# One branch per unit of expert weights, four hi and four lo buffers, and first loads in another order, in a two-layer hybrid decoder trunk

## The chip, the cores and the metric

The kernel runs on one core of one Trainium2 chip, all matrices in float32. The metric is the device time of one launch in microseconds. The core has five engines with their own instruction streams: PE (TensorE, matmuls), DVE (VectorE), ACT (ScalarE), POOL (GpSimd) and SP (SyncE), which here only issues DMA loads. An engine works through its stream in order; between engines there are semaphores only.

## The reference

Two layers. Each normalises x, mixes tokens (a gated delta rule beside a stick-breaking attention), and adds a feed-forward part: a dense SwiGLU in layer 0, a top-2-of-8 mixture of experts in layer 1. Shift, scale and gate of every part come from `silu(c) @ ada_w`. What matters here:

```python
D_MODEL, SEQ, DEPTH, D_FF, N_EXPERTS, TOP_K = 1024, 256, 2, 3584, 8, 2

def moe_swiglu(h, router_w, router_b, w1, w3, w2):
    logits = hf @ router_w + router_b
    top_logit, top_idx = lax.top_k(logits, TOP_K)
    top_w = jax.nn.softmax(top_logit, axis=-1)
    ...   # tokens gathered per expert in blocks of rows
    y = (jax.nn.silu(xb @ w1[e]) * (xb @ w3[e])) @ w2[e]
    ...   # weighted by top_w and summed back per token

def reference(x, c, ada_w, ...):
    c_act = jax.nn.silu(c)
    for l in range(DEPTH):
        mod = c_act @ ada_w[l] + ada_b[l]       # six parts: shift, scale, gate, twice
        x = x + gt1 * hybrid_mixer(rms_norm(x) * (1 + sc1) + sh1, ...)
        x = x + gt2 * (swiglu(h, ...) if l % 2 == 0 else moe_swiglu(h, ...))
    return rms_norm(x, final_norm)
```

## The kernel before

**Stages.** By the trace, the head (first loads, modulation of layer 0) lasts to about 42 us, the mixer of layer 0 to 385, the dense feed-forward to 640, the mixer of layer 1 to 995, routing and the first gather of tokens to 1013, the eight experts to 1950, and the end (last weighting, final norm, store) to 1970. A list scheduler sets the order of the instructions on each engine, by priorities that follow the program's text.

**Head.** ACT loads c (tile `csil`, L145, one float per element of the transfer, since c is laid out with its 1024 values as 128 x 8), takes silu, and loads some small tables: `rows` of layer 0 and of layer 1 (`setup`, L174 to L178) and the router's bias and weights (`rb`, `rw`, L1112 and L1113). SP loads the constants (`cst`, L157), x (L158) and eight pieces of 1 MiB of `ada_w` (L198, tiles `f`). PE multiplies each piece as it comes (L252, after silu of c is there), and what follows from the last piece opens the first large product (L503). Each DMA signals its end on one of eight semaphores that are handed out in turn (DMAHW0 to DMAHW7); a load whose semaphore is still held by an earlier load waits for that one.

**A unit of expert weights** is 1 MiB. Each expert has 42: 28 for up (w1 and w3, `up`), 14 for down (w2, `down`), in blocks of 1024, 1024, 1024 and 512 of the 3584 columns. For each unit SP loads `raw`, ACT casts it in two halves to a rounded copy `hl` (hi, L1267), and DVE subtracts to get the rest, `lo` (L1271). There are 7 buffers of raw (3 + 4), 4 of hi (3 + 1) and 4 of lo. `weights.group()` pops two units that are ready, after issuing two more loads and splits.

**Light and heavy.** An expert with at most 64 tokens is light: PE multiplies raw in float32 with 64 columns of tokens (`few`: L1372 in up, L1454 in down). Any other is heavy: PE multiplies hi by the tokens' hi and lo parts, and lo by their hi part (`heavy`: L1351, L1438, L1443). Which arm runs is decided on PE at run time by a flag per expert (`Light.arms`, L1219), with one branch for two units: 21 per expert. ACT casts and DVE subtracts in either case. Here experts 0, 2, 4 and 6 are heavy and 1, 3, 5 and 7 light; their stretches alternate. All eight flags are read into registers of PE by `values_load` (L1207) in one go ahead of the first gather (L1314, which multiplies the normalised tokens by a selection matrix `pe`).

**Around the units.** While expert e goes through up, expert e's earlier blocks go through down. Between them stand, for each block: `turned` (PE transposes L1412, ACT's copy `t2r` L1416, DVE's `t2r` L1417, and ACT's float32 copy `s`, called g32 in the code, L1420, from a pool `s32` of one buffer); the product of the two up halves on DVE (L1519); at each expert's start `begin`, with PE transposes (L1398), ACT's copy `pte` (L1400) and DVE's `ws` (L1402); for every second expert a gather (L1314, ACT L1325, L1330, DVE L1331). At the very end `finish_last` (L1488 on) weighs the last expert's result.

## Time and profile before

| | |
|---|---|
| runs | 1971.96, 1973.22, 1966.64 us (median 1971.96) |
| profiled execution | 1972.13 us, its span 1970.3 us |
| busy on PE, DVE, ACT | 1823.6, 1599.0, 1283.3 us |
| from HBM | 535 MB, 272 GB/s over the span |

The span is what the profiler saw between the first and the last instruction; the profiled execution's own time is 1.8 us more. Averages over the whole span mix stages with different limits, so the stages are read apart: busy time of each engine in each stretch, what an engine waited for in it, and the chain of waits at the head, at the start of the experts and at the end.

### The profile page before, as it was taken

What the parts mean: (1) busy time and instruction counts of PE and PEld (TensorE: products, weight loads), DVE (VectorE), ACT (ScalarE), POOL (GpSimd) and SP (SyncE); (2) the same over time, 40 slices, a digit from 0 to 9 for tenths busy, and PEclk for the clock granted to TensorE, in tenths of its full rate; (3) what the DMA queues carried; (4) which work ended last, traced back from release to release, by engine and by line L of the source; (5) the groups of instructions that cost most, each with busy time, mean ns of one, the idle gap of its engine ahead of it and who ended that gap; (6) DMA issues with size and microseconds to landing.
All of it is one profiled execution on the core that took longest, in us unless ns stands there. A gap on an engine that the chain in (4) does not pass through costs nothing.

```text
span 1970.3 us, 36475 instructions
## 1 busy us (share of the span) xinstructions
PE 1823.6 (93%) x14868; PEld 1412.8 (72%) x14868; DVE 1599.0 (81%) x1900; ACT 1283.3 (65%) x1842; POOL 80.0 (4%) x88
## 2 busy tenths in 40 slices
PE   5899999999999899999979988999889998899986
PEld 2889989999999789989968733686337863378522
DVE  3778678687666878588668898997989889898998
ACT  2765556454443665556477788877788687886885
POOL 0101000000000101000000002000020001000000
PEclk8999999999999999999989999999899998899998
DMA  8544447688773344555739999999999999999995
GB/s 279 168 155 144 143 153 235 214 288 279 246 260 95 127 153 131 162 171 193 259 140 377 365 402 348 380 369 365 381 355 383 367 370 365 370 374 368 377 403 232
DMA packets 220334, 539.24 MB, mean 274 GB/s; under 512 B 13602, under 2 KB 120548, under 8 KB 206052
## 3 DMA queue, kind: packets, MB, share of 16 engines
q1 hardware_dynamic: 215216, 536.02, 74.7%
q8 instruction: 148, 2.42, 0.5%
q10 hardware_dynamic: 4916, 0.35, 0.2%
q14 instruction: 54, 0.44, 0.1%
HBM read 535.27 MB, written 1.06 MB: 272 GB/s over the span
## 4 chain that ended last, share of the span: by engine, by line
PE 63%; DVE 18%; ACT 8%; issue 7%; DMA 4%; DVEq 0%; SPq 0%; ACTq 0%
PE g L1351 15%; PE g L379 7%; PE g L375 7%; PE g L377 7%; DVE lo L1271 7%; PE a L1438 4%; PE g L1372 3%; ACT hl L1267 3%; DMA raw<-in_moe_w_dram 2%; PE a L1454 2%; PE a L1443 2%; DVE t L627 2%; DVE hl L340 2%; ACT hl L339 1%; PE a L1055 1%
## 5 line engine op out<-in xcount | busy, mean ns | idle before, releaser
L1271 DVE TENSOR_TENSOR lo<-raw,hl 128x2048 fp32r<-128x2048 f32 (+1 forms) x338 | 754.1, 2272 | 46.5 <-ACT hl L1267 46.4
L1267 ACT CAST hl<-raw 128x1024 fp32r<-128x1024 f32 x672 | 657.3, 1052 | 26.0 <-DMA raw<-in_moe_w_dram 21.6
L340 DVE TENSOR_TENSOR hl<-raw,hl 128x1024 fp32r<-128x1024 f32 (+1 forms) x252 | 298.1, 1188 | 136.8 <-ACT hl L339 136.4
L339 ACT CAST hl<-raw 128x1024 fp32r<-128x1024 f32 (+1 forms) x252 | 256.8, 1022 | 201.3 <-PE g L379 134.0
L375 PE MATMUL g<-r,hl 128*128 128x256 f32 x1536 | 235.2, 293 | 6.6 <-ACT r L483 3.4
L377 PE MATMUL g<-r,hl 128*128 128x256 f32 x1536 | 228.6, 288 | 0.0
L379 PE MATMUL g<-r,hl 128*128 128x256 f32 x1536 | 223.9, 287 | 0.4 <-DVE hl L340 0.4
L1351 PE MATMUL g<-hl,r 128*128 128x512 f32 x896 | 222.9, 391 | 0.0
L375 PEld LDWEIGHTS g<-r,hl 128*128 128x128 f32 x1536 | 204.2, 194 | 15.2 <-ACT r L483 4.7
L1372 PE MATMUL g<-raw,x 128*64 128x512 f32 (+1 forms) x1024 | 212.1, 563 | 0.0
L377 PEld LDWEIGHTS g<-r,hl 128*128 128x128 f32 x1536 | 204.6, 195 | 3.0 <-issue 2.5
L379 PEld LDWEIGHTS g<-r,hl 128*128 128x128 f32 x1536 | 202.6, 194 | 2.6 <-issue 1.9
L1351 PEld LDWEIGHTS g<-hl,r 128*128 128x128 f32 x896 | 167.4, 188 | 37.0 <-ACT hl L1267 2.4
L1372 PEld LDWEIGHTS g<-raw,x 128*64 128x64 f32 x1024 | 71.5, 141 | 114.6 <-issue 104.2
L1454 PE MATMUL a<-raw,s 128*64 128x512 f32 x448 | 120.2, 684 | 3.6 <-ACT s L1420 3.2
L1351 PE MATMUL g<-lo,r 128*128 128x512 f32 x448 | 120.7, 391 | 0.5
L1416 ACT CAST t2r<-a 128x512 fp32r<-128x512 f32 x56 | 32.8, 585 | 113.1 <-PE a L1412 113.1
L1351 PEld LDWEIGHTS g<-lo,r 128*128 128x128 f32 x448 | 83.6, 188 | 20.0 <-DVE lo L1271 2.9
L210 DVE SCALAR_TENSOR_TENSOR f<-raw,csil,f 128x1024 f32<-128x1024 f32 x70 | 92.5, 1322 | 5.7 <-DMA raw<-in_ada_w_dram 5.2
L1438 PE MATMUL a<-hl,t2r 128*128 128x512 f32 x224 | 89.0, 397 | 1.7 <-ACT hl L1267 1.7
L1454 PEld LDWEIGHTS a<-raw,s 128*64 128x64 f32 x448 | 34.3, 157 | 74.5 <-issue 67.3
L1443 PE MATMUL a<-hl,t2r 128*128 128x512 f32 x224 | 87.5, 390 | 0.0
(334 smaller groups left out, 2211.6 us busy)
## 6 DMA issues: line engine op xcount, KB each, us to landing
raw<-in_moe_w_dram SPq DMA_DIRECT2D x334, 1024.0 KB, 7.0
raw<-in_w_in_dram SPq DMA_DIRECT2D x60, 1024.0 KB, 5.4
raw<-in_ffn_w_dram SPq DMA_DIRECT2D x42, 1024.0 KB, 5.8
raw<-in_ada_w_dram SPq DMA_DIRECT2D x40, 1024.0 KB, 5.3
f<-in_ada_w_dram SPq DMA_DIRECT2D x8, 1024.0 KB, 8.6
raw<-in_w_up_dn_dram SPq DMA_DIRECT2D x8, 1024.0 KB, 5.1
raw<-in_w_out_dram SPq DMA_DIRECT2D x8, 1024.0 KB, 5.0
raw<-in_w_up_sb_dram SPq DMA_DIRECT2D x4, 1024.0 KB, 5.1
```

The lines of the kernel that those rows point to most:

```text
L339: A.copy(hv, part)
L340: V.tensor_sub(lv, part, hv.bitcast(F32))
L375: T.matmul(pv[:, b, :], hv[:, k, :], xh[:, k, :], start=(k == 0), stop=False)
L377: T.matmul(pv[:, b, :], hv[:, k, :], xl[:, k, :], start=False, stop=False)
L379: T.matmul(pv[:, b, :], lv[:, k, :], xh[:, k, :], start=False, stop=(k == kc - 1))
L1267: A.copy(hi[:, h, :], raw[:, h, :])
L1271: V.tensor_sub(lo[:, h, :], raw[:, h, :], hi[:, h, :].bitcast(F32))
L1351: T.matmul(ps, x_[:, kk, :], w[:, k, 512 * b : 512 * b + 512], start=(kk == 0 and x_ is xh and w is hv), stop=(kk == KC - 1 and w is lv),)
L1372: T.matmul(banks[0][h, 0:half], x32[:, kk, :], w[:, k, half * i : half * i + half], start=(wide and kk == 0), stop=(kk == KC - 1), skip_gr ...
L1438: T.matmul(ye[nb], gh[:, gs], w[:, k, nw], start=(first and q == 0 and u == 0 and p == 0), stop=(last and u == 1 and p == 3),)
L1443: T.matmul(ye[nb], gl[:, gs], w[:, k, nw], start=False, stop=False)
L1454: T.matmul(ye[nb][h, :], g32[:, gs], w[:, k, 512 * nb : 512 * nb + 512], start=False, stop=(last and u == 1 and k == 1), skip_group_check= ...
```

## The change

In words, in the order of the program:

- c is loaded as 8 rows of 128 floats (`crow`), and PE turns it after silu; `cst` is the first load on SP, x follows two pieces of `ada_w` as before.
- The small `rows` loads of layer 1 and the router's two loads keep their place in the program (`tc.keep_in_program_order`) instead of being moved ahead by the scheduler; `rows` comes from a pool that is shared.
- At the experts' start seven loads are asked for ahead instead of five. The weights of the mixture (`mix`) are computed after the first gather instead of in `route`. The selection slots take one DVE operation instead of two.
- Each flag is read by a call in `begin(e)`.
- `take()` pops one unit, after one load and one split: each unit has a branch of its own (42 per expert). `step()`, which advances gathers and finishing work, runs after every second unit.
- `pte` and `ws` are made by `slots(e)` at the end of the expert's up phase, ahead of its last block's down, instead of at its start, from one buffer; `s32` has two.

```diff
@@ -89,7 +89,7 @@
     phase_m = dict(r8=4, r4=2, f8=7, f4=6, t2=6, i2=5, s2=4)
     banks_m = dict(g=2, s=2, a=3, v=1)
     phase_f = dict(raw2=3, hl2=3, r8=2, f4=4, t2=4, t2r=4)
-    phase_b = dict(raw2=4, hl2=1, lo=4, r4=6, x32=3, s32=1, t2=5, t2r=6, gt=1, xn=2, pe=2, pte=2)
+    phase_b = dict(raw2=4, hl2=1, lo=4, r4=6, x32=3, s32=2, t2=5, t2r=6, gt=1, xn=2, pe=2, pte=1)
 
     layout_b = dict(
         t2r=[P, 512], x32=[P, KC, P // 2], s32=[P, 512], xn=[P, 2, D], pe=[P, 512], r4=[P, KC, P], t2=[P, 512], pte=[P, S], gt=[P, D], raw2=[P, 2048],
...
@@ -142,10 +142,12 @@
 
 
     csil = pc.tile([P, KC], F32, tag="csil", name="csil")
-    nc.scalar.dma_start(csil, c_in[0].rearrange("(k p) -> p k", p=P))
-    A.activation(csil, csil, AF.Silu)
+    crow = pc.tile([KC, P], F32, tag="crow", name="crow")
+    nc.scalar.dma_start(crow, c_in[0].rearrange("(k p) -> k p", p=P))
+    A.activation(crow, crow, AF.Silu)
     cst = pc.tile([P, _CST.shape[1]], F32, tag="cst", name="cst")
     first = CST["i32"][1]
+    nc.sync.dma_start(cst[:, :first], cst_in[:, :first])
     C = {k: cst[:, a:b] for k, (a, b) in CST.items()}
     ident = C["ident"]
     ones = pc.tile([P, P], F32, tag="ones", name="ones")
@@ -154,7 +156,6 @@
     x = pc.tile([P, 2, D], F32, tag="x", name="x")
 
     def load_rows():
-        nc.sync.dma_start(cst[:, :first], cst_in[:, :first])
         nc.sync.dma_start(x, x_in[0].rearrange("(b p) d -> p b d", p=P))
 
...
 
     def setup(l):
 
-        rows = pc.tile([P, 2, P], F32, tag="rows", name=f"rows{l}")
+        pin = tc.keep_in_program_order if l else lambda ins: ins
+        rows = mk("t2", [P, 512])[:, 0 : 2 * P].rearrange("p (i c) -> p i c", c=P)
         G.memset(rows, 0.0)
-        nc.scalar.dma_start(rows[0:48, 0, :], ada_b[l].rearrange("(r p) -> r p", p=P))
...
+        pin(nc.scalar.dma_start(rows[0:48, 0, :], ada_b[l].rearrange("(r p) -> r p", p=P)))
+        pin(nc.scalar.dma_start(rows[48:56, 0, :], norm_mix[l].rearrange("(r p) -> r p", p=P)))
+        pin(nc.scalar.dma_start(rows[56:64, 0, :], norm_ffn[l].rearrange("(r p) -> r p", p=P)))
+        pin(nc.scalar.dma_start(rows[64:65, 0, :], dn_out_norm[l : l + 1, :]))
+        pin(nc.scalar.dma_start(rows[0:96, 1, :], conv_w[l].rearrange("j (r p) -> (j r) p", p=P)))
...
     def ada_first(l, mods):
 
         cs = mk("r4", [P, 4 * S])[:, : 32 * KC].rearrange("p (k c) -> p k c", c=32)
-        V.tensor_copy(cs, csil.unsqueeze(2).broadcast_to([P, KC, 32]))
...
@@ -240,8 +241,12 @@
                 raws[m, q] = ada_load(l, m, q, "f8")
                 if len(raws) == 2:
                     load_rows()
-                if len(raws) == 5:
+                if len(raws) == 4:
                     rest = setup(0)
+        ps = bank("a")
+        T.transpose(ps[:, 0:KC], crow, ident[0:KC, 0:KC])
+        V.tensor_copy(csil, ps[:, 0:KC])
+        V.tensor_copy(cs, csil.unsqueeze(2).broadcast_to([P, KC, 32]))
...
-            nc.scalar.dma_start(rb, router_b[j : j + 1, :].partition_broadcast(P))
-            nc.scalar.dma_start(rw[:, 0], router_w[j].rearrange("(k p) n -> p k n", p=P))
+            tc.keep_in_program_order(nc.scalar.dma_start(rb, router_b[j : j + 1, :].partition_broadcast(P)))
+            tc.keep_in_program_order(nc.scalar.dma_start(rw[:, 0], router_w[j].rearrange("(k p) n -> p k n", p=P)))
...
         light = Light(rt[:, 5, 0])
-        wgt = sm([P, 2, 2])
...
-        V.tensor_add(wt, wt, tmp)
-        return oa, wt, pos, light
+        def mix():
+
+            wgt = sm([P, 2, 2])
...
+            V.tensor_tensor(tmp, tmp, wgt[:, :, 1:2].broadcast_to([P, 2, NE]), ALU.mult)
+            V.tensor_add(wt, wt, tmp)
+
...
             V.tensor_copy(self.int, self.flag)
-            self.back = pc.tile([P, NE], F32, tag="back", name="back")
-            V.tensor_scalar(self.back, self.flag, -float(P // 2), None, ALU.mult)
-            self.regs = [
-                nc.values_load(self.int[0:1, e : e + 1], engines=[mybir.EngineType.PE], min_val=0, max_val=1)
-                for e in range(NE)
-            ]
+            self.regs = {}
 
         def slots(self, e):
 
             t = mk("t2", [P, 512])[:, 0:P]
-            V.tensor_scalar(t, C["iota"], P // 2 - 0.5, self.back[:, e : e + 1], ALU.is_gt, ALU.mult)
-            V.tensor_add(t, t, C["iota"])
+            V.scalar_tensor_tensor(t, foldr, self.flag[:, e : e + 1], C["iota"], ALU.mult, ALU.add)
             return t
+
+        def fetch(self, e):
+            self.regs[e] = nc.values_load(
+                self.int[0:1, e : e + 1], engines=[mybir.EngineType.PE], min_val=0, max_val=1
+            )
...
-        def group(self):
-
-            self.load(2)
+        def take(self):
+
+            self.load(1)
             self.split(4)
-            return [self.ready.popleft() for _ in range(2)]
...
-            for u0 in range(0, KC // kc, 2):
-                units = weights.group()
-                light.arms(e, lambda: few(u0, units), lambda: heavy(u0, units))
+            for u in range(KC // kc):
+                unit = weights.take()
+                light.arms(e, lambda: few(u, *unit), lambda: heavy(u, *unit))
                 weights.after = None
-                weights.load(5)
+                weights.load(4)
                 yield
             yield banks
 
         st = {}
 
         def begin(e):
+            light.fetch(e)
+            st[e] = []
+
+        def slots(e):
 
             ps = bank("a")
             for b in range(2):
@@ -1400,7 +1410,7 @@
             A.copy(pte, ps[:, 0:S])
             ws = sm([P, 1])
             V.tensor_copy(ws, ps[:, S : S + 1])
-            st[e] = (pte, ws, [])
+            return pte, ws
...
+            for m in range(n // 256):
+                unit = weights.take()
+                light.arms(e, lambda: few(m, *unit), lambda: heavy(m, *unit))
+                weights.load(4)
                 yield
...
         def hidden(e, n, late):
 
-            p1 = up(e, n)
-            next(p1)
-            g = turned(late[3]) if late else None
-            step()
-            for banks in p1:
-                step()
+            for i, banks in enumerate(up(e, n)):
+                if i == 1:
+                    g = turned(late[3]) if late else None
+                if i % 2:
+                    step()
             ss = [mk("t2", [P, 512]) for _ in banks]
             for s1, ps in zip(ss, banks):
                 A.activation(s1, ps, AF.Silu)
-            for banks in up(e, n):
-                step()
+            for i, banks in enumerate(up(e, n)):
+                if i % 2:
+                    step()
             for s1, ps in zip(ss, banks):
                 V.tensor_mul(s1, s1, ps)
             return ss, g
...
         gath = {}
         drain([gather(0)])
+        merge.begin()
         late = None
         for e in range(NE):
             begin(e)
             for f, n in blocks:
                 ss, g = hidden(e, n, late)
                 if late:
-                    for _ in down(*late[:3], *g):
-                        step()
                     if late[1:3] == blocks[-1]:
-                        steps.append(finish(late[0]))
+                        ends = slots(late[0])
+                    for i, _ in enumerate(down(*late[:3], *g)):
+                        if i % 2:
+                            step()
+                    if late[1:3] == blocks[-1]:
+                        steps.append(finish(late[0], *ends))
                         step()
                 late = (e, f, n, ss)
...
             gt = None
+            mixed = False
+
+            def begin(self):
+                if not self.mixed:
+                    self.mixed = True
+                    mix()
 
             def start(self):
                 if self.gt is None:
```

The arms' products are the same, cut in two; `down` is changed as `up` is.

SP at the kernel's head, before. The names after DMA are the tile and its source; in brackets stands which semaphores the issue waits for.

```order
L198 DMA f_6_100<-in_ada_w_dram 128x2x1024
L198 DMA f_7_102<-in_ada_w_dram 128x2x1024
L157 DMA cst<-in_cst_dram 128x160 [waits DMAHW3_49]
L158 DMA x<-in_x_dram 128x2x1024 [waits DMAHW4_49]
L198 DMA f_8_106<-in_ada_w_dram 128x2x1024 [waits DMAHW6_49]
L198 DMA f_9_108<-in_ada_w_dram 128x2x1024 [waits DMAHW2_49]
L198 DMA f_10_110<-in_ada_w_dram 128x2x1024 [waits DMAHW4_49]
L198 DMA f_11_119<-in_ada_w_dram 128x2x1024 [waits DMAHW5_49]
L198 DMA f_12_121<-in_ada_w_dram 128x2x1024 [waits DMAHW6_49]
L198 DMA f_13_123<-in_ada_w_dram 128x2x1024 [waits DMAHW7_49,DMAHW1_49,PE_49]
```

The same place now:

```order
L150 DMA cst<-in_cst_dram 128x160
L200 DMA f_6_102<-in_ada_w_dram 128x2x1024
L200 DMA f_7_104<-in_ada_w_dram 128x2x1024
L159 DMA x<-in_x_dram 128x2x1024 [waits DMAHW2_49]
L200 DMA f_8_107<-in_ada_w_dram 128x2x1024 [waits DMAHW3_49]
L200 DMA f_9_109<-in_ada_w_dram 128x2x1024 [waits DMAHW4_49]
L200 DMA f_11_118<-in_ada_w_dram 128x2x1024 [waits DMAHW5_49]
L200 DMA f_12_120<-in_ada_w_dram 128x2x1024 [waits DMAHW6_49]
L200 DMA f_13_122<-in_ada_w_dram 128x2x1024 [waits DMAHW7_49]
L200 DMA f_14_124<-in_ada_w_dram 128x2x1024 [waits DMAHW0_49,PE_49]
```

`cst` no longer waits, and the router's loads, which took two of the semaphores on which the pieces of `ada_w` waited, are not among the loads of the head any more.

PE between the routing and the first expert, before: TENSOR_LOAD reads a flag (eight in all, each followed by two ISA rows), a_123.. are the gather's sums.

```order
L1176 MATMUL a_12187<-rt,ones 128x8 x2
L1207 TENSOR_LOAD lighti [waits DVE_49]
L1207 ISA x2
...
L1314 MATMUL a_12313<-pe_12296,xn_12288 128x256 [waits DVE_49,PE_49,Activation_49]
...
L1314 MATMUL a_12367<-pe_12296,xn_12289 128x256
L1393 MATMUL a_12385<-rt,pe_12296 128x1 [waits Activation_49]
...
L1398 MATMUL a_12385<-cst,pe_12296 128x128 x2
L1219 COMPARE_AND_BRANCH
```

The same place now:

```order
L1181 MATMUL a_12197<-rt,ones 128x8 x2
L1222 TENSOR_LOAD lighti [waits DVE_49]
L1222 ISA x2
...
L1322 MATMUL a_12229<-pe_12214,xn_12206 128x256 [waits DVE_49,PE_49,Activation_49]
...
L1322 MATMUL a_12283<-pe_12214,xn_12207 128x256
L1222 TENSOR_LOAD lighti
L1222 ISA x2
...
L1227 COMPARE_AND_BRANCH
```

Two flag reads stay ahead of the gather's 32 products; the other six stand behind them, all ahead of the first branch. The matmuls for `pte` and `ws` are gone from here.

ACT in the last expert's last block, before (CAST hl is half a unit's hi, COPY s is g32):

```order
L1416 CAST t2r_21837<-a_21832 128x512 [waits PE_49]
L1267 CAST hl_21749<-raw_21660 128x1024 [waits DMAHW4_49,DVE_49]
L1267 CAST hl_21749<-raw_21660 128x1024
L1267 CAST hl_21787<-raw_21662 128x1024 [waits DMAHW5_49,DVE_49]
L1267 CAST hl_21787<-raw_21662 128x1024 [waits DMAHW6_49]
L1219 UNCONDITIONAL_BRANCH
L1267 CAST hl_21793<-raw_21740 128x1024 [waits DMAHW7_49,DVE_49]
L1267 CAST hl_21793<-raw_21740 128x1024 [waits DMAHW0_49]
L1420 COPY s_2917_21841<-a_21832 128x512 [waits DVE_49,PE_49]
```

The same place now:

```order
L1426 CAST t2r_21991<-a_21986 128x512 [waits PE_49]
L1227 UNCONDITIONAL_BRANCH
L1410 CAST pte_22002<-a_21997 128x256 [waits PE_49]
L1275 CAST hl_21901<-raw_21790 128x1024 [waits DMAHW4_49,DVE_49]
L1275 CAST hl_21901<-raw_21790 128x1024
L1430 COPY s_2917_21995<-a_21986 128x512 [waits DVE_49]
L1275 CAST hl_21923<-raw_21818 128x1024 [waits DMAHW5_49,Activation_49]
```

`pte` now comes right after `t2r`, and g32 stands behind two casts instead of six.

## Rows read from the trace of the kernel before

**Rows 1.** Busy time by stretch: start:end, length, engines (instructions), clock, DMA share, GB/s.

```profile
42.00:385.00 343.00, 329.61 (x4475) 307.88 (x4476) 259.03 (x503) 201.97 (x383) 19.85 (x19) 0.98 0.52 171
640.00:995.00 355.00, 335.70 (x4519) 308.20 (x4518) 265.15 (x526) 202.74 (x391) 20.44 (x20) 0.98 0.51 169
...
1127.30:1244.60 117.30, 101.93 (x462) 42.13 (x461) 110.73 (x82) 96.40 (x121) 10.24 (x8) 0.91 0.98 376
1244.60:1364.90 120.30, 119.87 (x542) 96.10 (x542) 107.73 (x66) 92.24 (x107) 0.00 (x0) 1.00 0.98 368
1364.90:1483.60 118.70, 101.90 (x461) 42.09 (x461) 110.76 (x82) 96.35 (x121) 10.17 (x8) 0.91 0.97 371
...
1603.90:1722.50 118.60, 102.21 (x461) 41.93 (x461) 110.74 (x82) 96.32 (x121) 10.17 (x8) 0.91 0.97 372
...
1842.80:1950.00 107.20, 92.50 (x422) 36.22 (x422) 106.13 (x66) 90.70 (x105) 0.00 (x0) 0.95 0.98 388
```

**Rows 2.** The chain of waits in the head: start us, us, what.

```profile
0.75 9.03 DMA csil<-in_c_dram
...
10.65 0.58 ACTq L1112
...
11.28 8.80 DMA rw<-in_router_w_dram
...
22.37 13.17 DMA f<-in_ada_w_dram
...
42.00 1.83 PE a L503 x7
```

**Rows 3.** Busy time by stretch in the head, columns as in rows 1.

```profile
20.00:25.00 5.00, 3.57 (x8) 0.49 (x8) 3.36 (x18) 0.26 (x2) 0.00 (x0) 0.59 0.74 250
...
30.00:35.60 5.60, 4.29 (x26) 0.89 (x20) 0.00 (x0) 0.00 (x0) 0.00 (x0) 1.00 1.03 404
```

**Rows 4.** PE's timeline in the head: start, us, operation, idle before it and releaser.

```profile
19.94 3.63 PE L252 MATMUL g<-f,r 128*32 128x512 f32 x8 [5.55 <-DMA f<-in_ada_w_dram]
...
35.59 1.91 PE L252 MATMUL s<-f,r 128*32 128x512 f32 x8 [0.67 <-DMA f<-in_ada_w_dram]
```

**Rows 5.** PE's timeline at the experts' start.

```profile
1006.72 5.76 PE L1314 MATMUL a<-pe,xn 128*128 128x256 f32 x32 [6.51 <-issue]
...
1012.86 2.08 PE L1351 MATMUL g<-hl,r 128*128 128x512 f32 x8
```

**Rows 6.** The instructions of L1207: min/median/max ns, first and last start.

```profile
L1207 PEldq TENSOR_LOAD <-lighti x8: 297/302/492, 1000.9 to 1005.9; - x8
```

**Rows 7.** DVE's timeline at the experts' start.

```profile
1001.86 1.10 DVE L1296 TENSOR_SCALAR pe<-t,rt 128x128 fp32r<-128x128 f32 x4
```

**Rows 8.** Waits in the second light expert, 1364.9:1483.6: us in total, times, longest.

```profile
ACT t2r L1416 <- PE a L1412: 9.1, 3, 4.3
...
DVE lo L1271 <- ACT hl L1267: 7.3, 6, 2.3
...
ACT hl L1267 <- DMA raw<-in_moe_w_dram: 4.0, 5, 2.1
...
ACT pte L1400 <- PE a L1398: 2.4, 1, 2.4
```

**Rows 9.** DVE's timeline at the end of the first light expert.

```profile
1226.85 11.14 DVE L1271 TENSOR_TENSOR lo<-raw,hl 128x2048 fp32r<-128x2048 f32 x5 [1.73 <-ACT hl L1267]
```

**Rows 10.** The branches (L1219): min/median/max ns, first and last start.

```profile
L1219 PEldq COMPARE_BRANCH  x252: 65/179/413, 1010.9 to 1950.7; - x126
```

**Rows 11.** PE's timeline in the first light expert.

```profile
1131.30 7.09 PE L1372 MATMUL g<-raw,x 128*64 128x512 f32 x32
```

**Rows 12.** PE's groups in the second heavy expert, 1244.6:1364.9: busy, mean ns, idle before.

```profile
L1351 PE MATMUL g<-hl,r 128*128 128x512 f32 x224 | 55.8, 391 | 0.0
```

**Rows 13.** Timelines of PE and DVE at the end.

```profile
1950.64 3.65 PE L1454 MATMUL a<-raw,s 128*64 128x512 f32 x16 [3.25 <-ACT s L1420]
...
1954.33 1.41 DVE L1488 SCALAR_TENSOR_TENSOR t<-a,sm,gt 128x512 f32<-128x512 f32 x2 [1.14 <-PE a L1454]
```

134 lines of the change are left out of this document (63 added, 71 removed).

## The prediction

> **What bounds the kernel now.** I read the stretches first, then what the engines wait for in each kind of stretch, then the chain of waits where the program has a seam. The two mixers and the dense stage are bound by PE: 329.61 of 343 us and 335.70 of 355 us [rows 1]. The diff does not change what they compute. The experts alternate between two limits. In a heavy stretch PE is busy for 119.87 of 120.30 us; nothing that DVE, ACT or the loads save there can shorten it. In a light stretch PE has time (101.93 of 117.30 us) and DVE is next to the limit: 110.73 of 117.30, 110.76 of 118.70, 110.74 of 118.60, and 106.13 of 107.20 us in the last one. The loads run at 371 to 388 GB/s in those stretches [rows 1], against 404 GB/s where many large loads stand in the queues [rows 3], so they are near a limit too, but not on it. What can be had in a light stretch is therefore DVE's idle time: 6.6, 7.9, 7.9 and 1.1 us, 23.5 us in all. DVE's wait list says whom it waits for there: the hi casts of ACT (7.3 us), and ACT in turn waited for PE's transposes (9.1 us in three waits, and 2.4 us for `pte`) and for loads (4.0 us) [rows 8]. Beside that there are three seams where one chain holds everything: the head to 42 us [rows 2], the start of the experts [rows 5], and the end [rows 13].
>
> **The head.** The chain of the head begins with the load of c, one float at a time: 9.03 us. SP's `cst` waits for a semaphore that is free only after it. Later a piece of `ada_w` stands behind the router's load, which held a semaphore for 8.80 us, and the last piece, issued at 22.37, lands 13.17 us later, at 35.54; the first large product starts at 42.00 [rows 2], 6.46 us after that. Meanwhile the loads moved 250 GB/s between 20 and 25 us, and 404 GB/s between 30 and 35.6 when nothing held SP back [rows 3]. In the new order `cst` waits for nothing, the router's loads are gone from the head, and x and the third piece wait only for the first two pieces. The head must bring nine loads of 1 MiB and 80 KB, 9.5 MB: at 404 GB/s 23.5 us from the first issue at 0.75, so 24.3 with no hole. As x waits for the first piece to land, I count the first two pieces at the slower 250 GB/s (8.4 us instead of 5.2): 27.5. Against 35.54 that is 8 us, with 11 as the upper end. PE multiplies a piece in 1.91 us warm, but in 3.63 us where it had idled before [rows 4]; some cold pieces could eat 1 us of it. The turn of c on PE and two more DVE copies stand beside loads that are still on their way. I take **-7.0** (5 to 11 gained). Since layer 0 is bound by PE from then on, the gain is carried to the end. The five `rows` loads of layer 1, now issued on ACT ahead of the dense stage, and the router's two, issued at the start of the second mixer, cost up to 0.58 us of issue each on ACT (the router's bias) [rows 2], where ACT is busy for 202.74 of 355 us [rows 1]: 0, up to 4 if all seven stood on the path.
>
> **The start of the experts.** PE reads eight flags one after the other: the first starts at 1000.9 and the last at 1005.9 [rows 6], so 0.71 us each, and idles 6.51 us until the gather starts at 1006.72, though DVE's selection `pe` was done by 1002.96 [rows 5, 7]. In the new order two reads stand ahead of the gather and six behind it. The gather could start at some 1002.9; its 32 products and what follows took 6.14 us to the first expert's product at 1012.86 [rows 5]. If the six reads (4.3 us) came wholly after the gather's 5.76 us, the start would be at 1013, no sooner than now; if they ran while PE still worked through queued products, at 1009.1, 3.8 sooner. PE's branches leave no gap between products (below), so PE's sequencer is ahead of the products and some of the reads should be hidden: **-2.0** (0 to 3.8). Note that the flags are not read one by one, expert after expert, since the scheduler puts all eight ahead of the first branch. The mixture's weights leave the path of DVE here, which waits for nothing then: 0. Seven loads ahead instead of five meet seven buffers of raw, so the eighth waits as before: 0.
>
> **The units.** Half of the idle time of DVE in the light stretches has a cause that the change touches. First, `pte`: at the end of a light expert ACT waits for PE's transposes, and DVE then 1.73 us for its hi cast [rows 9]. `pte` now follows `t2r` in another place: 1.7 x 3 = 5.2 us. Second, with units taken singly, three units instead of two are split ahead of each branch, and the gather's steps stand two units apart; of the other 17.2 us of idle time in the three full light stretches (22.4 less 5.2) I take 4.8, as much as the waits for loads (4.0 in one stretch) and the three waits for `t2r` leave likely. Together **-10**. The bounds: -22.4 if DVE never idled there, which would ask for 44.04 MB in 110.7 us, 398 GB/s, just under the 404 of rows 3; and +6 if `pte`, behind `t2r`, waits for as long as the longest wait for `t2r` (4.3 us instead of 2.4, three times). The two buffers of `s32` change nothing in a heavy stretch. DVE saves an operation for each expert's slots, under 0.3 us in a stretch: in the range.
>
> **The branches.** 168 are added. On PE's sequencer a branch takes 0.179 us in the median and 0.413 at most [rows 10], but that ran beside the products: in the first light expert 32 products stand in one row of 7.09 us with a branch between them [rows 11], and the 336 products of L1351 in a heavy expert had an idle time of 0.0 before them (two thirds of them in [rows 12]). All that PE idled in that stretch, 0.43 us for 21 branches, is 0.02 us each; 84 more in the heavy stretches would be 1.7 us. ACT and DVE have a jump for each branch as well, and DVE's five subtractions in a row took 11.14 us, 2.23 each, with jumps among them [rows 9]. **+0.5** (0 to 1.7).
>
> The Trainium skill speaks against this part: "Runtime: NRT & Kernel Launch", section "Instruction fetch mechanics", has it that branching breaks the sequential prefetch and that a taken branch whose target lies outside the window forces a fetch before execution goes on. The rows above show no such stall at 21 branches per expert, while the skipped arm is halved by the change. By that rule the sum would end as in the third rival.
>
> **The end.** The last block's 16 products wait 3.25 us for g32, which ACT copies after six casts; DVE's first weighting then waits 1.14 us for PE at 1954.33 [rows 13]. g32 now stands behind two casts. PE could end 3.2 us sooner, but DVE has its last subtractions in the queue until 1953.2, so only the 1.14 us and a little of the block's earlier product are to be had: **-1.3** (0 to 3).
>
> **The sum** against the profiled execution's own 1972.13 us (the median of the runs is 1971.96, so nothing has to be moved): 1972.13 - 7.0 - 2.0 - 10 + 0.5 - 1.3 = 1952.3.
>
> **The rivals.** First, *the light stretches do not shorten*: the loads bring 371 to 376 GB/s because the memory gives no more while ACT and DVE also work, and the idle time of DVE merely moves. For it speaks a DMA share of 0.97 to 0.98 [rows 1]; against it the last light stretch at 388. Time: 1972.13 - 7.0 - 2.0 + 0.5 - 1.3 = 1962.3. Second, *the head's gain is not kept*, because the first pieces land no sooner (semaphores are handed out in turn, and x now waits for the first piece): 1952.3 + 7 = 1959.3. With the first rival as well: 1969.3. Third, ending on the other side, *the branches come to light*: an arm of a heavy unit has 12 products, 2.7 us, instead of 24, and if PE's sequencer no longer gets ahead of it, each of the 168 heavy branches shows. At the median of 0.179 us that is 30 us, at the maximum 69: 1982 to 2021. It decides from 20 / 168 = 0.12 us each. In the light stretches PE's own slack of 15 us hides as much. Against it stand rows 11 and 12. Fourth, *ACT's new order stalls it longer* in the light stretches, +6 in place of -10: 1968.
>
> **How the numbers follow.** A run of this kernel can tell 0.3%, 5.9 us, from no change: faster is below 1966, slower above 1978. The forecast has 0.52, all faster. The first rival has 0.22 (0.19 faster, 0.03 the same), the second 0.08 (0.07 and 0.01), both together 0.06 (0.01 and 0.05), the third 0.07 (0.02 the same, 0.05 slower), the fourth 0.05 (0.03 the same, 0.02 slower). So faster 0.79, the same 0.14, slower 0.07. The time is the forecast's, 1952.3. The range goes from 1936, where most of the light stretches' idle time is gone, to 1972, which takes in the first, second and fourth rivals and leaves out the third; about 0.15 lies outside.
>
> **What would show it.** The head: the first large product at 34 to 36 us instead of 42, and the mixers as long as before. The start: the first expert's products some 11 us after the last routing product instead of 13. The light stretches: 115 us each, with DVE idle for 4 to 5 us and no wait for `pte`, at 380 GB/s or more. The heavy stretches: 120.3 us with PE idle for under 1 us; a gap of 0.1 us or more at each branch would make the third rival true. The end: PE's last 16 products no longer wait for g32. Wrong would be above all a light stretch of 117 us or more, or a heavy one above 121.

## The result and the profile after

The changed kernel took 1947.45 us (median of 4 runs, 1945.89 to 1952.21) against 1971.3 us before: a ratio of 0.9886, 95% interval 0.9861 to 0.9912. The forecast was 1952.3, in a range of 1936 to 1972. (The title also names four hi and four lo buffers. Both kernels have these; the pools that change among the experts are `s32`, from one buffer to two, and `pte`, from two to one.) The profiled execution took 1945.89 us, its span 1944.0, so 26.2 us less than the profiled execution before. By stage, from the first product of each to the first of the next (the last one to the end of the span):

| stage | before, us | after, us | difference |
|---|---|---|---|
| head, to the first large product | 42.00 | 34.57 | -7.4 |
| layer 0 and the mixer of layer 1, to the last routing product | 957.9 | 956.6 | -1.2 |
| routing to the first expert | 13.0 | 10.3 | -2.7 |
| heavy experts 0, 2, 4, 6 | 475.2 | 477.9 | +2.7 |
| light experts 1, 3, 5 | 354.6 | 338.4 | -16.2 |
| light expert 7 and the end | 127.6 | 126.2 | -1.4 |

The stretches of the changed kernel, with the columns of [rows 1]:

```profile
34.57:378.00 343.43, 329.99 (x4474) 307.89 (x4475) 259.08 (x502) 202.00 (x383) 20.41 (x19) 0.98 0.52 169
...
1117.30:1229.20 111.90, 98.56 (x461) 41.12 (x460) 107.52 (x78) 93.34 (x118) 6.26 (x8) 0.94 0.98 377
1229.20:1350.00 120.80, 119.65 (x541) 96.14 (x540) 111.13 (x68) 96.14 (x110) 0.00 (x0) 1.00 1.00 385
1350.00:1464.10 114.10, 99.42 (x461) 41.02 (x460) 107.27 (x78) 93.27 (x118) 5.89 (x8) 0.93 0.95 367
...
1585.10:1697.50 112.40, 97.03 (x462) 40.48 (x461) 107.55 (x78) 93.37 (x118) 6.20 (x8) 0.95 0.97 374
```

Two things differ from [rows 1]. DVE idles 4.4, 6.8 and 4.9 us in the three light stretches instead of 6.6, 7.9 and 7.9. And DVE works 3.2 to 3.5 us less in a light stretch (107.3 to 107.6 instead of 110.7) and 3.4 us more in a heavy one (111.13 instead of 107.73): 40 subtractions end in a light stretch and 44 in a heavy one, where there were 42 in each. Work has moved to where DVE has time, and the heavy stretch pays for it with 0.5 us (0.1 to 0.7 in the three full ones). PE idles 1.15 us in the heavy stretch shown instead of 0.43, and nearly all of it in one wait, for a subtraction that the light stretch left behind:

```profile
PE g L1358 <- DVE lo L1279: 1.1, 1, 1.1
```

The waits of the second light expert, beside [rows 8]:

```profile
ACT t2r L1426 <- PE a L1422: 8.7, 2, 5.9
DVE lo L1279 <- ACT hl L1275: 6.7, 8, 2.1
...
ACT hl L1275 <- DMA raw<-in_moe_w_dram: 3.9, 5, 2.2
```

The wait of ACT for `pte` (2.4 us in [rows 8]) is gone; the others have hardly changed.

The start of the experts on PE, beside [rows 5], and the flag reads, beside [rows 6]:

```profile
993.94 6.41 PE L1322 MATMUL a<-pe,xn 128*128 128x256 f32 x32 [2.37 <-DVE mosti L1596]
1001.52 0.73 PE L1358 MATMUL g<-hl,r 128*128 128x512 f32 x2 [1.16 <-ACT t L1333]
```

```profile
L1222 PEldq TENSOR_LOAD <-lighti x8: 299/303/495, 992.2 to 1000.5; - x8
```

PE idles 2.37 us ahead of the gather instead of 6.51, so the gather starts 2.73 us after the last routing product (991.21) instead of 6.86: 4.1 us gained. At the first expert's product 2.7 of them are left. The row puts its wait of 1.16 us down to ACT, but the flag reads end later. The last read starts at 1000.5 and is done with its two steps at 1001.17; only then comes the first branch:

```profile
L1227 PEldq COMPARE_BRANCH  x504: 65/176/444, 1001.2 to 1922.4; - x168
```

It ends at 1001.46, and the product starts at 1001.52, while the ACT row ended at 1001.41. In the kernel "pairs" (below) ACT was done 0.27 us ahead of that product, and the branch 0.05 us, so the reads and the branch are what ends last. At the end, beside [rows 13]:

```profile
1917.65 8.80 PE L1462 MATMUL a<-raw,s 128*64 128x512 f32 x40
...
1928.03 1.40 DVE L1496 SCALAR_TENSOR_TENSOR t<-a,sm,gt 128x512 f32<-128x512 f32 x2
```

PE's last products run in one row without a wait for g32, and DVE's first weighting follows its last subtraction without idling.

### The profile page after: what moved, and what is told of

Its sections match the earlier page's. It is cut to its first block, busy times and chain, and to the rows that moved or that the text cites. A ratio compares the mean times of both kernels' runs of the same rounds, so it can differ in the third digit from the quotient of the medians.

```text
span 1944.0 us, 36722 instructions
## 1 busy us (share of the span) xinstructions
PE 1810.3 (93%) x14869; PEld 1407.9 (72%) x14869; DVE 1598.7 (82%) x1892; ACT 1287.4 (66%) x1842; POOL 72.6 (4%) x89
## 4 chain that ended last, share of the span: by engine, by line
PE 64%; DVE 18%; ACT 7%; issue 5%; DMA 4%; SPq 1%; ACTq 0%; DVEq 0%
PE g L1358 13%; PE g L380 7%; PE g L384 7%; PE g L382 7%; DVE lo L1279 6%; PE g L1378 5%; PE a L1447 5%; DMA raw<-in_moe_w_dram 3%; PE a L1452 2%; PE a L1462 2%; ACT hl L1275 2%; DVE t L632 2%; DVE hl L345 2%; PE a L1060 1%; PE a L1061 1%
## 5 line engine op out<-in xcount | busy, mean ns | idle before, releaser
L1462 PE MATMUL a<-raw,s 128*64 128x512 f32 x448 | 110.4, 635 | 0.0
L632 DVE SCALAR_TENSOR_TENSOR t<-t,conv,t 128x255 f32<-128x255 f32 (+2 forms) x144 | 61.8, 476 | 26.2 <-ACT t L627 26.1
```

Source lines behind the costliest of these rows:

```text
L1462: T.matmul(ye[nb][h, :], g32[:, gs], w[:, k, 512 * nb : 512 * nb + 512], start=False, stop=(last and m == n // 256 - 1 and k == 1), skip_g ...
```

## The experiments

Twelve kernels were run. A profile gives each stage apart, so beside the median there is one figure that the head does not touch: from the first expert's product to the end of the span. "Its before" is the kernel before, timed beside each one.

| kernel | median, us | its before | ratio (95%) | head ends | experts to end |
|---|---|---|---|---|---|
| before | | | | 42.0 | 957.4 |
| changed | 1947.45 | 1971.30 | 0.9886 (0.9861 to 0.9912) | 34.6 | 942.5 |
| pairs | 1954.64 | 1969.33 | 0.9917 (0.9886 to 0.9947) | 39.8 | 945.9 |
| unit_alone | 1970.09 | 1969.33 | 1.0009 (0.9996 to 1.0022) | 42.4 | 957.3 |
| halves | 1996.14 | 1969.33 | 1.0135 (1.0110 to 1.0160) | 39.7 | 989.1 |
| flags_first | 1951.41 | 1969.33 | 0.9916 (0.9892 to 0.9939) | 36.4 | 945.9 |
| s32_1 | 1954.88 | 1970.23 | 0.9921 (0.9903 to 0.9938) | 36.8 | 946.8 |
| pte_first | 1961.35 | 1970.23 | 0.9953 (0.9935 to 0.9971) | 39.2 | 957.2 |
| c_elements | 1950.24 | 1970.23 | 0.9898 (0.9880 to 0.9916) | 35.1 | 946.3 |
| no_pin | 1951.78 | 1970.23 | 0.9902 (0.9884 to 0.9920) | 36.8 | 946.3 |
| pte_late | 1961.49 | 1969.92 | 0.9957 (0.9945 to 0.9970) | 42.1 | 949.1 |
| cst_late | 1945.35 | 1969.92 | 0.9874 (0.9859 to 0.9890) | 34.3 | 945.9 |
| pool_cast | 1948.38 | 1969.92 | 0.9892 (0.9876 to 0.9907) | 35.2 | 946.2 |
| pool_pairs | 1949.80 | 1969.92 | 0.9900 (0.9886 to 0.9914) | 34.7 | 942.6 |

Four kernels hold the changed kernel's experts unaltered (c_elements, no_pin, cst_late, pool_cast) and took 945.9 to 946.3 us there; the changed kernel's own profile, with 942.5, is 3.5 us below them. So 3 to 4 us of this figure is what one profile can differ from another.

### Is it the branch per unit?

The changed kernel with one branch for two units:

```diff
-            for u in range(KC // kc):
-                unit = weights.take()
-                light.arms(e, lambda: few(u, *unit), lambda: heavy(u, *unit))
+            for u0 in range(0, KC // kc, 2):
+                units = weights.group()
+                light.arms(e, lambda: [few(u0 + i, *u) for i, u in enumerate(units)],
+                           lambda: [heavy(u0 + i, *u) for i, u in enumerate(units)])
...
```

> The changed kernel with one branch for two units again (two loads, two splits, one pop of two, as before); all else as changed. Theory A, which the two traces suggest: a branch per unit lets the subtractions (lo) fall one unit further behind by the end of a light expert and get one further ahead by the end of a heavy one, so that two of a light expert's 42 subtractions are done in heavy stretches, where DVE has time. Then the pairs bring back 42 subtractions to each stretch, light stretches of 116 to 119 us instead of 112 to 114, heavy ones of 120.3, and some 1960 us. Theory B, by the prediction: the light stretches gained by the other place of pte and fewer waits of ACT. Then they stay at 112 to 115 us and the time at 1947 to 1950.

The light stretches took 112.8, 117.1 and 113.9 us, the heavy ones that follow 120.7, 119.2 and 119.3, and it was 945.9 us from the first expert to the end: as much as the kernels with the branch per unit. The light stretches are some 3 us longer in sum than theirs (343.8 against 339.6 to 341.1), and the heavy ones some 5 us shorter. The median lies between the times of the two theories. The head of this profile ended at 39.8 us, though its instructions are those of the changed kernel; that is 5.3 of the 9.7 us by which this execution is longer than the changed kernel's profiled one (see the head, below).

The other way round, the kernel before with the branch per unit alone (`take()` and the arms of the change, no more):

```diff
-            for u0 in range(0, KC // kc, 2):
-                units = weights.group()
-                light.arms(e, lambda: few(u0, units), lambda: heavy(u0, units))
+            for u in range(KC // kc):
+                unit = weights.take()
+                light.arms(e, lambda: few(u, *unit), lambda: heavy(u, *unit))
...
-                weights.load(5)
+                weights.load(4)
...
```

> The kernel before with the branch per unit alone (one load, one split, one pop, gathers advanced after every second unit); pte, s32, flags, head as before. Theory A: 40 subtractions in a light stretch and 44 in the heavy ones that follow, light stretches of 112 to 115 us, heavy ones 0.5 us longer, some 1957 us. Theory B: light stretches of 117 to 119 us as before, some 1970 us.

Nothing was gained: 1.0009, with an interval that holds 1. Two of its stretches, a light one and the heavy one behind it:

```profile
1125.60:1244.80 119.20, 100.97 (x461) 41.12 (x460) 109.99 (x81) 96.20 (x121) 5.96 (x8) 0.93 0.96 366
1244.80:1364.40 119.60, 119.49 (x540) 96.27 (x538) 108.99 (x67) 92.64 (x107) 0.00 (x0) 1.00 0.99 372
```

One subtraction has moved (41 end in the light stretch, 43 in the heavy one), but DVE idles 9.2 us instead of 6.6: moving work is no gain while DVE still waits. Theory A of these two runs fell.

Last, both with the head's spread taken out (by the edit of pool_cast, below):

```diff
-        A.copy(wv[:, :, 0:n], raw)
+        G.tensor_copy(wv[:, :, 0:n], raw)
...
-                unit = weights.take()
-                light.arms(e, lambda: few(u, *unit), lambda: heavy(u, *unit))
+                units = weights.group()
+                light.arms(e, lambda: [few(u0 + i, *u) for i, u in enumerate(units)],
+                           lambda: [heavy(u0 + i, *u) for i, u in enumerate(units)])
...
```

> The same with one branch for two units: what the branch per unit is worth once pte is late, with the head's spread taken out. Theory: nothing that can be measured, since the changed kernel's experts took 942.5 us and those of three kernels with the same experts 946 us, and pairs 945.9; pool_cast and this within 3 us. Rival: the branch per unit lets one subtraction more per light expert fall into the heavy one; then this is 3 to 6 us slower than pool_cast.

1949.80 against 1948.38 us, with intervals that overlap. Light and heavy stretches of pool_cast (a branch per unit), then of pool_pairs:

```profile
1116.90:1229.10 112.20, 97.06 (x462) 40.50 (x461) 107.55 (x78) 93.45 (x118) 6.27 (x8) 0.95 0.97 373
1229.10:1350.30 121.20, 119.92 (x540) 96.13 (x538) 111.08 (x68) 96.09 (x110) 0.00 (x0) 1.00 1.00 385
```

```profile
1116.40:1230.30 113.90, 98.78 (x462) 40.77 (x461) 111.35 (x80) 97.05 (x122) 8.30 (x8) 0.96 0.99 385
1230.30:1349.60 119.30, 119.30 (x542) 96.14 (x540) 107.24 (x66) 91.17 (x107) 0.00 (x0) 1.00 0.98 374
```

This shows the trade: the branch per unit takes 1.7 us off this light stretch, since 3.8 us of DVE's work goes to the heavy one, and the heavy one is 1.9 us longer, since PE now idles there for 1.3 us where it did not idle at all. Over this pair the sum is nothing. Over all experts the profile of pool_pairs is 3.6 us shorter (942.6 against 946.2), which is no more than two profiles can differ.

### Late `pte`, and the second buffer of g32

The changed kernel with one buffer for g32:

```diff
-    phase_b = dict(..., s32=2, ..., pte=1)
+    phase_b = dict(..., s32=1, ..., pte=1)
```

> The changed kernel with one buffer of s32 (g32) again. The kernel before with a branch per unit alone gained nothing (lights of 119 us), and the changed kernel with pairs kept two thirds of the gain in the light stretches (113 to 117), so the rest of the change carries it: pte and ws made late, or the second buffer for g32. Theory pte: s32 does not matter; light stretches of 112 to 114 us as in the changed kernel, 1947 to 1951 us; at the very end g32 waits for PE and up to 2 us are lost. Theory s32: the light stretches go to 117 to 119 us, some 1960 us.

Light stretches of 113.0, 114.0 and 114.3 us and 946.8 us in all: the second buffer is not what shortens them. (The median is 7.4 us above the changed kernel's; in the profile 2.2 us of the difference stand in the head, 2.3 between the head and the routing, and 4.3 in the experts, where it lies 0.5 above the four kernels named above.)

`pte` and `ws` made at each expert's start again (with one buffer of g32, for want of room):

```diff
         def begin(e):
             light.fetch(e)
             st[e] = []
+            made[e] = slots(e)
...
-                        ends = slots(late[0])
+                        ends = made.pop(late[0])
...
```

> The changed kernel with pte and ws made at each expert's start, as before, with two buffers of pte and, for want of room, one of s32; to be read against the run with one buffer of s32 alone. Theory pte: ACT waits 2 to 2.5 us for PE's transposes near the end of each light expert again, DVE idles 7 to 8 us instead of 4.5 to 7, and light stretches are 3 to 5 us longer than with late pte; some 1957 us. Theory s32: no more than 1 us of difference from the run with one buffer of s32.

Light stretches of 118.8, 119.2 and 119.2 us, and 957.2 us from the first expert to the end: all that the experts had gained is lost. Beside s32_1, which differs in this edit alone, that is 10.4 us; but this profile is of the slowest of the kernel's four executions (1966.32; the others took 1959.96 to 1961.47), and by the medians the edit costs 6.5 us (1961.35 against 1954.88). The timelines at the end of the first light expert, first PE, then ACT and DVE, of this kernel:

```profile
1213.94 1.95 PE L1424 MATMUL a<-cst,t 128*128 128x128 f32 x8 [6.69 <-DVE t L1529]
...
1223.01 0.42 PE L1410 MATMUL a<-cst,pe 128*128 128x128 f32 x2
```

```profile
1223.46 0.37 ACT L1412 CAST pte<-a 128x256 fp32r<-128x256 f32 x1 [3.52 <-PE a L1410]
```

```profile
1223.86 0.16 DVE L1414 COPY sm<-a 128x1 f32<-128x1 f32 x1 [1.18 <-ACT pte L1412]
1225.75 7.05 DVE L1279 TENSOR_TENSOR lo<-raw,hl 128x2048 fp32r<-128x2048 f32 x3 [1.73 <-ACT hl L1275]
```

And PE, then ACT, of the changed kernel at the same place:

```profile
1206.27 1.95 PE L1422 MATMUL a<-cst,t 128*128 128x128 f32 x8 [6.68 <-DVE t L1527]
```

```profile
1223.43 0.59 ACT L1426 CAST t2r<-a 128x512 fp32r<-128x512 f32 x1
1224.05 0.37 ACT L1410 CAST pte<-a 128x256 fp32r<-128x256 f32 x1
```

The transposes for the early `pte` stand in PE's stream between two units of the last up block. PE came late to them, since it had waited 6.69 us for the product of the up halves on DVE; ACT waited 3.52 us for PE, and DVE, whose next subtraction needs ACT's cast, 2.9 us for ACT. The rows read as a ring of three engines: DVE's queue holds up PE, PE holds up ACT, and ACT holds up DVE. PE waits as long for DVE in the changed kernel (6.68 us); what is gone there is the copy by which ACT, and through it DVE, had to wait for PE further on. Late `pte` follows right behind `t2r`, and at this place ACT waits for neither. That the place of `pte` is the cause is shown by this run and the next; that each link of the ring passes the wait on is read from the rows, and no link was taken out alone.

The edit alone, in the kernel before:

```diff
         def begin(e):
+            st[e] = []
+
+        def slots(e):
...
+                    if late[1:3] == blocks[-1]:
+                        ends = slots(late[0])
                     for _ in down(*late[:3], *g):
                         step()
                     if late[1:3] == blocks[-1]:
-                        steps.append(finish(late[0]))
+                        steps.append(finish(late[0], *ends))
```

> The kernel before with one edit: pte and ws are made late, ahead of the last block's down, as in the change; pairs, flags, head, one buffer of s32 as before. Theory: this edit alone carries the gain of the experts, since with it undone all eight experts take as long as before (957 us from the first expert to the end in both), and a branch per unit without it gained nothing. Then light stretches of 113 to 117 us, 946 to 950 us from the first expert's product to the end, and some 1961 us. Rival: late pte needs the branch per unit to work; then light stretches stay at 117 to 119 us and the time at 1968 to 1971.

0.9957, 8.4 us, and 949.1 us from the first expert to the end instead of 957.4. So late `pte` alone carries some 8 of the 11 to 15 us that the experts gain, without a branch per unit. Its light stretches took 118.5, 116.6 and 114.3 us, some 5 us less in sum, and its heavy ones 472.0 us in sum instead of 475.3: three of the four ran with PE never idle. Why the first light stretch gained nothing there stays open, as does what brings the last 3 us (pairs, which adds g32's second buffer, the later mixture's weights and the shorter slots, has them).

### What a branch costs

Each unit's products in two halves, with a branch each:

```diff
-                light.arms(e, lambda: few(u, *unit), lambda: heavy(u, *unit))
+                for part in (range(0, kc // 2), range(kc // 2, kc)):
+                    light.arms(e, lambda: few(u, part, raw), lambda: heavy(u, part, hv, lv))
...
```

> The changed kernel with two branches per unit, each over half of the unit's products (672 branches in all, 336 more). If a branch is free as long as PE has products queued (6 products, 1.4 us, in a heavy arm): heavy stretches of 120 to 121 us, some 1947 us. Rival, branches cost once arms are short: at 0.02 us for each of 168 more heavy ones 3 us (1951), at the sequencer's median of 0.18 us 30 us (1978), heavy stretches of 128 us.

49 us more than the changed kernel: heavy stretches of 124.9, 127.6, 127.6 and 129.2 us, light ones of 114.5, 118.0 and 115.2. By the rival's sum the sequencer's 0.18 us for each branch would do for the heavy ones. But PE's timeline in a heavy stretch does not show it; six products stand between two branches here:

```profile
1259.69 1.07 PE L1358 MATMUL g<-hl,r 128*128 128x512 f32 x4
1260.60 0.61 PE L1358 MATMUL g<-lo,r 128*128 128x512 f32 x2
1261.05 1.07 PE L1358 MATMUL g<-hl,r 128*128 128x512 f32 x4
1261.96 0.61 PE L1358 MATMUL g<-lo,r 128*128 128x512 f32 x2
```

From one branch's first product to the next one's is 1.36 and 1.36 us (1259.69, 1261.05, 1262.41), six products at 0.227: no gap at a branch. The stretch that these rows come from (1245.3 to 1372.9) is 6.8 us longer than the changed kernel's. PE's idle time has 2.9 of them (4.05 instead of 1.15); the other 3.9 stand in PE's busy time (123.55 instead of 119.65), where short rows of different products now alternate. Its waits:

```profile
ACT hl L1275 <- PE g L1358: 15.8, 10, 3.5
DVE lo L1279 <- ACT hl L1275: 13.5, 13, 4.1
...
PE g L1358 <- DVE lo L1279: 2.3, 2, 1.9
```

ACT waits 15.8 us for PE to give hi buffers back (0.7 us in the same stretch of the changed kernel), DVE for ACT, and PE for some of their units. So the price of this finer cut does not show as gaps at the branches in these rows. That it comes from how the engines' work falls between the branches is what the waits suggest; which reordering does it was not tried apart, and stays open.

### The start of the experts

All eight flags read in one go ahead of the gather:

```diff
-            self.regs = {}
+            self.regs = [nc.values_load(self.int[0:1, e : e + 1], engines=[mybir.EngineType.PE], ...)
+                         for e in range(NE)]
...
```

> The changed kernel with all eight flags read in one go ahead of the gather, as before. Theory: six of the eight reads ran while PE still worked through the gather, so reading them first puts some 4 us between routing and gather; the first expert starts 12 to 13 us after the last routing product instead of 10.3, and the time is 2 to 3 us longer, 1950. Rival: the start gained from the earlier selection matrix on DVE and the moved mixture's weights; then the first expert still starts 10 to 11 us after routing, and the time is 1947.

From the last routing product to the first expert's it took 12.3 us (993.11 to 1005.42) instead of 10.3, and 13.0 before. PE's idle time ahead of the gather is back:

```profile
999.96 5.62 PE L1323 MATMUL a<-pe,xn 128*128 128x256 f32 x32 [6.49 <-issue]
1005.42 0.86 PE L1359 MATMUL g<-hl,r 128*128 128x512 f32 x3
```

So 2.0 of the 2.7 us are the flags. The other 0.7 lies behind the gather, not ahead of it: the gather starts 6.85 us after the last routing product, as before (6.86), and from its start to the first expert it takes 5.46 us instead of 6.14. The products for `pte` and `ws`, which held 0.54 us there before (1012.32 to 1012.86), have moved away. The selection matrix, which DVE has ready earlier now, shows no gain of its own in this run.

### The head

Three kernels undo one edit each: c by elements, the small loads no longer held back, `cst` behind two pieces.

```diff
-    crow = pc.tile([KC, P], F32, tag="crow", name="crow")
-    nc.scalar.dma_start(crow, c_in[0].rearrange("(k p) -> k p", p=P))
-    A.activation(crow, crow, AF.Silu)
+    nc.scalar.dma_start(csil, c_in[0].rearrange("(k p) -> p k", p=P))
+    A.activation(csil, csil, AF.Silu)
...
```

> The changed kernel with c loaded one float at a time again (and silu on it in place), cst still first, the router's and layer 1's small loads still held back. The head of the changed kernel ended at 34.6 us in one profile and at 36.4 to 39.8 in profiles of kernels with the same head, so its end is not steady. Theory: c's 1024 small pieces (9 us before) delay the first products of the ada pieces to 10 us and the eighth load with them; the head ends at 38 to 42 us, 2 to 5 us later than with rows. Rival: the small load of a few columns of w_in, which now waits 14 to 17 us behind the large loads, sets the end, and c costs nothing: 35 to 40 us as before.

```diff
-        pin = tc.keep_in_program_order if l else lambda ins: ins
+        pin = lambda ins: ins
...
-            tc.keep_in_program_order(nc.scalar.dma_start(rb, ...))
-            tc.keep_in_program_order(nc.scalar.dma_start(rw[:, 0], ...))
+            nc.scalar.dma_start(rb, ...)
+            nc.scalar.dma_start(rw[:, 0], ...)
```

> The changed kernel with the router's loads and layer 1's rows free to be moved ahead by the scheduler. Theory: they go back into the head, hold two semaphores and put small loads in the way: the head ends at 40 to 43 us as before, 1953 to 1955 us. Rival: the order of cst and c made the gain; then the head ends at 35 to 40 us and the time stays at 1947 to 1950.

```diff
-    nc.sync.dma_start(cst[:, :first], cst_in[:, :first])
...
     def load_rows():
+        nc.sync.dma_start(cst[:, :first], cst_in[:, :first])
         nc.sync.dma_start(x, x_in[0].rearrange("(b p) d -> p b d", p=P))
```

> The changed kernel with cst loaded behind two pieces of ada_w again. c by elements and the loads left free each kept the head at 35 to 37 us in their profiles, so neither alone carries its gain. Theory: cst ahead carries it, since the turn of c and of the small rows on PE wait for cst; behind two pieces it lands some 5 us later, and the head ends at 39 to 42 us. Rival: each of the edits alone is enough to free the stream of pieces, since all that is needed is that no piece waits for a slow small load; then the head ends at 35 to 40 us, as in the changed kernel's family.

Their heads ended at 35.1, 36.8 and 34.3 us: each of the three edits can be undone alone and the gain stays. So no single one of them is the cause. What they have in common is that in each of them no piece of `ada_w` waits long for a semaphore that a slow small load holds. SP had issued the last of the eight pieces by 22.8 us before, by 12.5 in the changed kernel, and by 13.4 to 15.0 in these three. SP's waits on small loads in the head, before:

```profile
SPq L198 <- DMA rw<-in_router_w_dram: 8.6, 1, 8.6
SPq L157 <- DMA rows<-in_norm_mix_dram: 8.4, 1, 8.4
```

In the changed kernel, then in no_pin:

```profile
SPq L159 <- DMA t<-in_ada_b_dram: 3.9, 1, 3.9
```

```profile
SPq L329 <- DMA rw<-in_router_w_dram: 8.9, 1, 8.9
```

In no_pin the router's load holds its semaphore as long as before, but now a load of `w_in` waits for it (L329), not a piece of `ada_w`. With `cst` behind two pieces, PE's first products come later, but it catches up while the pieces still come:

```profile
10.11 0.24 PE L247 MATMUL a<-cst,crow 8*128 8x8 f32 x1 [10.11 <-DMA cst<-in_cst_dram]
...
34.33 1.83 PE L508 MATMUL a<-r,hl 128*128 128x256 f32 x7 [3.44 <-DVE t L489]
```

The head is not steady, though: with one and the same code it ended at 34.6 us in the profile of the changed kernel, 36.4 and 36.8 in two others, and 39.2 to 39.8 in three. ACT's timeline of the changed kernel, then of pairs, differs in one load:

```profile
10.22 0.30 ACT L499 CAST hl<-t 128x128 fp32r<-128x128 f32 x1 [5.88 <-DMA t<-in_w_in_dram]
```

```profile
20.26 0.30 ACT L499 CAST hl<-t 128x128 fp32r<-128x128 f32 x1 [15.91 <-DMA t<-in_w_in_dram]
```

It is the load of 16 columns of `w_in`, 64 KB in 1024 pieces of 64 bytes. It was issued at 3.2 us in both, and landed after 7 us or after 17, among the large loads. The normalising of x stands behind its cast on ACT, and in pairs PE then waits for the normalised x:

```profile
26.17 0.47 PE L475 MATMUL v<-cst,f 128*128 128x128 f32 x1 [5.92 <-DVE f L451]
```

With the cast on POOL instead:

```diff
-        A.copy(wv[:, :, 0:n], raw)
+        G.tensor_copy(wv[:, :, 0:n], raw)
```

> The changed kernel with the cast of the few columns of w_in (narrow_weights) on POOL instead of ACT. In five of seven profiles with the changed head, ACT waited 13 to 16 us for this small load behind the large ones, and the normalising of x stood behind it; there the head ended at 36.4 to 39.8 us, against 34.6 to 36.8 where the load came after 6 us. Theory: with the cast off ACT, the head ends at 34 to 36 us in every run, and the median falls by 1 to 4 us to 1944 to 1947, with less spread. Rival: the pieces themselves come later in those runs, and the small load is only a witness; then 1947 to 1951 as the changed kernel.

In this profile the load took 17.22 us again, but the work on x began at 13.62, and the head ended at 35.2. (In pool_pairs it ended at 34.7, but there the load took 7.1 us, so it says nothing on this.) The runs lie within 2.9 us (1947.01 to 1949.95; the changed kernel's within 6.3), but the median, 1948.38, is no lower than the changed kernel's. So the wait is shown, and an edit that takes it away; a gain over the changed kernel's median is not. No kernel of these is faster than it beyond the intervals.

## Why the prediction was right, and where it was not

**The time** was 4.9 us below the forecast, inside the range, and clear of the times of all four rivals (1959 and more).

**The head**, -7.0, gave -7.4 in the profile. That small loads hold semaphores for which the pieces wait was read rightly, and for the router's load it holds by SP's waits (8.6 us); for `cst` and x it named the wrong loads. By the same waits it was not c's load that held up `cst`, but a load of `rows` of 4 KB (8.4 us), and with c loaded by elements again the head still ended at 35.1. In the new order x waits 3.9 us for a small load of `ada_b`, not for the first piece. The gain rests on none of the three edits alone. Nor is it steady: in the five other profiles with the same head it was 2.2 to 5.6 us, so that the profile hits -7 so closely is in part luck. The forecast did not see that the load of `w_in`'s columns can cost up to 5 us in the new order.

**The start**, -2.0, gave -2.7, of which the flags 2.0. That PE's sequencer runs ahead of its products was right in part: the six reads behind the gather began at 997.09, while PE worked through the gather until 1000.36, but they and the first branch lasted until 1001.46 and are what the first expert's product waited for last. How much sooner it could start without them is not shown, since ACT's work there ended only 0.05 us earlier.

**The light stretches**, -10, gave -16.2 in the profile, -13 to -15 in the profiles of the kernels with the same experts (for pool_cast 339.6 against 354.6). The terms that went wrong are both parts of the sum. Units taken singly, 4.8 us, are nothing: 957.3 against 957.4 us for the experts in the kernel before, and 945.9 against 945.9 to 946.3 in the changed one. Late `pte` was given the idle time behind it on DVE, 1.73 us three times, 5.2. Alone in the kernel before it took some 5 us from the light stretches, but by +1.2, -2.0 and -4.3, and 3.3 from the heavy ones, which the forecast had put at nothing. In the changed kernel, undone, it costs 2.9 us of DVE's idle time at that place and lets one subtraction less move into the heavy stretch, 2.2 us, so some 5 us for each light stretch, not 1.7; the heavy ones give 5 us of it back, and 10.4 us are left by the profiles, 6.5 by the medians. The row of 1.73 us was only the last link of a chain. That the sum for the experts (-10, +0.5 and -1.3) comes near the -11 to -15 measured is luck: a term that was nothing made up for one that was too small. Two of the forecast's signs did not come either: the light stretches' loads ran at 367 to 377 GB/s, not at 380 or more, and PE idled 1.1 to 1.2 us in a heavy stretch, not under 1. The first rival's premise, that the memory gives no more than 371 to 376 GB/s while ACT and DVE work, is answered by the heavy stretches at 384 to 385.

**The branches**, +0.5 for PE, were read rightly at this size: no gap at a branch even with six products between two of them. The heavy stretches became 2.7 us longer in the profile all the same, by the work that moved in; the forecast said that nothing which DVE saves can shorten a heavy stretch, and overlooked that PE stands still when the light stretch before leaves more of DVE's work behind. The third rival, that branches come to light, did not happen here. The finer cut of halves costs 49 us, but the rows read show no gap at a branch on PE, which speaks against the third rival's mechanism there too. As to the rule of the Trainium skill ("Runtime: NRT & Kernel Launch", "Instruction fetch mechanics") on a stall at taken branches, no stall shows here where products are queued: PE's products follow each other at 0.227 us across the branches of halves. Whether a target here lies outside that page's window, no run shows.

**The end**, -1.3, gave -1.4 for the whole last stage, and the rows after agree with its mechanism: no wait for g32, and DVE's last subtraction is the bound. That stage holds the last expert too, and it took 126.2 to 128.3 us in the profiles of the kernels with the same experts, so the number is no more than agreement.

**Layer 0 and the mixer** of layer 1 took 1.2 us less, which the forecast put at 0. In the profiles of all the kernels these stages took between 955.0 and 959.0 us, with no pattern by their edits, so this is no finding.

## What to carry to other kernels

Where two engines wait in turn, look for a third one that passes the wait on: the price of a badly placed small copy can be more than the last wait that a row shows (here 6 to 10 us instead of 1.7 us three times). A change that bears one idea's name may live by a side edit: undo each part alone, and add the likely one alone, before the idea is carried on. And moving work from a stage that is bound by an engine to one that is not gains only if the second stage really has room for it when it arrives, and if the first one does not go on waiting for something else. Where a row names the engine that ended a wait, compare the end of that engine's work with the end of the branch or the flag read that came before.

## What was not expected of the hardware

A load of 64 KB in pieces of 64 bytes, issued at 3.2 us beside loads of 1 MiB, landed after 7 us in two executions and after 14 to 17 us in others with the same loads. A branch on PE, whose own record lasts 0.18 us in the median, showed no gap between products even when only 1.36 us of products lay between two branches. Where PE had nothing queued, at the first expert, the branch and the flag reads ahead of it stood in the open: the product started 0.05 to 0.06 us after the branch's end. The loads reached 385 GB/s over a whole heavy stretch, with a DMA share of 1.00, while PE was busy for 119.65 of 120.8 us.
